# Second-stretch counting between the sort steps, warm matmuls ahead of the first bins, and all unpacking ahead of the block loop, in a graph attention kernel

## The chip, the cores and the metric

One core of a Trainium2 chip. The metric is the device time of one execution in microseconds (us), median of several runs. The span of a trace is about 1.9 us shorter than the time of the same run. The granted clock is the share of its full clock that TensorE was given; in the traces its record holds only 0.5 and 1.0, and a mean of these is given over a span.

## The reference, cut to what matters

A graph attention layer: 4096 nodes, 50000 edges, 4 heads, 64 features in and out.

```python
for h in range(n_heads):
    x_proj[h] = x @ weight[h]
    edge_scores[h] = (x_proj[h, src] * att_src[h]).sum(-1) + (x_proj[h, dst] * att_dst[h]).sum(-1)
edge_scores = np.where(edge_scores > 0, edge_scores, 0.2 * edge_scores)
# per head and destination: sum of exp(score) * x_proj[src], over the sum of exp(score) (+ 1e-8)
```

The kernel sorts the edges by source and then by destination, so that 125 destinations (one block, 33 of them) lie in a known stretch of each of 8 sorted runs. It fetches a window of each stretch, unpacks the keys into source and destination numbers (`tb`), spreads these over all partitions (`bc`), compares them to one-hot matrices (`oh`), gathers with matmuls on them (`ex`, `xs`), and sums with matmuls (`val`, `acc`).

## The kernel before

`V`, `S`, `G`, `T` are VectorE, ScalarE, GpSimd, TensorE. The part that the change touches is the hand-over from the second sort to the loop over blocks (tiny helpers cut, `...` marks cuts, the comments are added here):

```python
def unpack(self, i, *engs):                      # one window of 8 blocks: keys -> bins
    V.tensor_scalar(out=t[:, 1, :], in0=self.win[:, i, :], ...)      # source
    V.tensor_scalar(out=t[:, 0, :], in0=self.win[:, i, :], ...)      # destination
    (S.copy if i == 0 else V.tensor_copy)(out=tb[:, 1, :], in_=t[:, 1, :])
    V.tensor_scalar(out=tb[:, 0, :], in0=t[:, 0, :], scalar1=boff[:, i:i + 1], ...)
    ...                                          # stores of tb to memory, for the bc loads
...
group(so2, Lent(), ws1[:], spy)                  # second sort; then bounds(): counts -> ws2, we2
win = Windows(cst, ws2[:])                       # five indirect fetches on GpSimd
whole(so2, we2, (1 << FINE) - 1, 1)
for c in range(len(CH)):
    blocks.onehot(0, *CH[c])
    blocks.gather(0, c)
win.unpack(0, nc.sync, nc.sync)
for b in range(2, 5):
    blocks.load(b)                               # bc(2)..bc(4): loads of the stored bins
blocks.weights(0)
blocks.values(0)                                 # val: one product of 128 x 4096
for c in range(len(CH)):
    blocks.spread(1, c, win.tb[:, 0], lambda t: NT + t, S.copy if c < 2 else V.tensor_copy)
    if c == 1:
        blocks.onehot(1, *CH[0])
for c in (1, 2):
    blocks.onehot(1, *CH[c])
blocks.sums(0, -1); blocks.gather(1, 0); blocks.sums(0, 0); blocks.gather(1, 1); blocks.gather(1, 2)
win.unpack(1, nc.sync, nc.sync)
longest(so2, Lent(), (ws1, we1), (ws2, we2))     # longest stretch of all partitions
n1, n2 = room(0, EL), room(1, L)                 # two counts into registers of EVERY engine
blocks.sums(0, 1)
blocks.weights(1)
blocks.onehot(2)
blocks.run(1, {i - 1: lambda i=i: win.unpack(i, nc.sync, nc.sync) for i in range(2, NI)})
...
with tc.If((n1 > W1) | (n2 > W2)):               # fallback for long stretches: not taken here
    ...
```

## Time and profile before

| | before |
|---|---|
| time, median of 4 runs | 296.28 us (296.14 to 296.56) |
| span of the profiled run | 294.9 us, mean granted clock 0.859 |
| last result computed (`res`, VectorE) | 288.71 us |
| from there to the end of the span | 6.20 us |
| `oh` of block 2 starts | 130.87 us |

The last row divides the hand-over from the loop.

### The profile page before, as it was taken

The numbers are of one execution on the slowest core, as the hardware profiler recorded it, in microseconds if no ns is written. First come the engines' busy times: TensorE is split into PE (matmuls) and PEld (weight loads), VectorE is DVE, ScalarE is ACT, GpSimd is POOL, SyncE is SP. The second block draws the span as 40 slices with busy tenths as digits, with TensorE's granted clock in tenths as the row PEclk, the third lists the DMA queues.
The fourth block names the chain that finished last, engine by engine and source line by source line (L and its number), as shares of the span: only waits on it lengthen the run. The fifth ranks groups of instructions, "written<-read, shape, count | busy, mean of one in ns | idle before, by whom it ended". The sixth has DMA issues, their size and how long they took to land.

```text
span 294.9 us, 8453 instructions
## 1 busy us (share of the span) xinstructions
PE 202.5 (69%) x3541; PEld 193.8 (66%) x3541; DVE 260.6 (88%) x504; ACT 186.0 (63%) x361; POOL 27.6 (9%) x78
## 2 busy tenths in 40 slices
PE   0001899960000007669999999999999999999980
PEld 0000599960000005559899999999999999999980
DVE  5999999995599999679999999999999999999960
ACT  2960710040599935857778787878787778777850
POOL 7882000001100002400000000000000000000000
PEclk9999975555555555899999999999999999999996
DMA  3025000000100001295768756876578657864012
GB/s 109 0 53 109 0 2 0 0 1 37 36 0 0 0 0 40 66 392 185 242 258 307 254 185 234 292 273 197 217 289 285 197 206 282 293 203 183 8 37 59
DMA packets 13326, 40.75 MB, mean 138 GB/s; under 512 B 3120, under 2 KB 8912, under 8 KB 9312
## 3 DMA queue, kind: packets, MB, share of 16 engines
q1 hardware_dynamic: 10768, 37.91, 36.4%
q10 hardware_dynamic: 1808, 1.56, 2.3%
q0 software_dynamic: 704, 0.66, 1.0%
q8 instruction: 30, 0.49, 0.7%
q14 instruction: 16, 0.13, 0.1%
HBM read 35.08 MB, written 5.05 MB: 136 GB/s over the span
## 4 chain that ended last, share of the span: by engine, by line
PE 50%; DVE 40%; issue 3%; DMA 2%; ACT 2%; DVEq 0%; POOL 0%; POOLq 0%; ACTq 0%
PE acc L545 17%; DVE sA L210 13%; DVE sB L210 12%; PE ps L494 10%; PE pf L606 6%; PE ps L492 6%; PE ps L498 5%; PE acc L538 4%; DVE val L520 2%; DVE sB L239 1%; DVE oh L471 1%; DMA eS<-in_edge_index_dram 1%; ACT xs L502 1%; DMA raw<-gat_sorted,wi 1%; DVE sA L199 1%
## 5 line engine op out<-in xcount | busy, mean ns | idle before, releaser
L502 ACT CAST xs<-ps 128x1200 bf16<-128x1200 f32 (+1 forms) x99 | 104.0, 1051 | 0.0
L520 DVE TENSOR_TENSOR val<-xs,wv 128x4096 bf16<-128x4096 bf16 (+1 forms) x34 | 75.4, 2220 | 1.0 <-ACT xs L502 1.0
L545 PE MATMUL acc<-xs,val 128*128 128x125 bf16 x1024 | 61.8, 218 | 1.9 <-issue 1.5
L494 PE MATMUL ps<-adb,oh 128*128 128x136 bf16 x528 | 62.6, 225 | 0.0
L492 PE MATMUL ps<-xa,oh 128*128 128x72 bf16 x528 | 59.9, 198 | 2.6 <-DVE oh L471 2.2
L545 PEld LDWEIGHTS <-val 128*128 128x128 bf16 x1056 | 58.8, 98 | 2.4 <-issue 1.7
L494 PEld LDWEIGHTS <-oh 128*128 128x128 bf16 x528 | 49.8, 99 | 0.5 <-issue 0.4
L492 PEld LDWEIGHTS <-oh 128*128 128x128 bf16 x528 | 47.6, 99 | 2.9 <-DVE oh L471 2.9
L500 ACT ACTIVATE ex<-ps 128x96 bf16<-128x96 f32 (+1 forms) x99 | 25.0, 252 | 33.0 <-PE ps L498 32.9
L471 DVE TENSOR_SCALAR oh<-bc,pF 128x4096 bf16<-128x4096 bf16 (+2 forms) x37 | 42.4, 1146 | 0.3 <-ACT bc L458 0.3
L210 DVE TENSOR_TENSOR sA<-sB 128x256 f32<-128x256 f32 (+2 forms) x104 | 37.2, 399 | 1.7
L210 DVE TENSOR_TENSOR sB<-sA 128x256 f32<-128x256 f32 (+2 forms) x98 | 35.1, 399 | 1.6
L498 PE MATMUL ps<-xa,oh 128*128 128x72 bf16 x528 | 33.7, 199 | 0.0
L292 PE MATMUL cnt_ps<-sgn,sel 128*128 128x17 f32 (+1 forms) x6 | 1.7, 390 | 41.9 <-ACT sgn L284 41.9
L292 PEld LDWEIGHTS cnt_ps<-sgn,sel 128*128 128x128 f32 x6 | 1.4, 318 | 42.0 <-issue 42.0
L498 PEld LDWEIGHTS <-oh 128*128 128x128 bf16 x528 | 26.7, 100 | 0.1
L474 DVE TENSOR_SCALAR oh<-bc,pF 128x2048 bf16<-128x2048 bf16 (+2 forms) x37 | 25.5, 689 | 0.0
L395 PEld LDWEIGHTS at_ps<-uv,xT 64*128 64x128 f32 x130 | 24.8, 298 | 0.3 <-issue 0.3
L395 PE MATMUL at_ps<-uv,xT 64*128 64x4 f32 x130 | 24.9, 328 | 0.0
L606 PE MATMUL pf<-Wbd,aT 128*128 128x128 f32 x132 | 22.7, 294 | 2.7 <-ACT aT L602 0.8
L281 ACT ACTIVATE junk<-kr,nb 128x512 f32<-128x512 f32 x33 | 23.8, 722 | 1.1
L606 PEld LDWEIGHTS pf<-Wbd,aT 128*128 128x128 f32 x132 | 17.3, 191 | 4.5 <-issue 3.4
(139 smaller groups left out, 213.6 us busy)
## 6 DMA issues: line engine op xcount, KB each, us to landing
bc<-gat_bins SPq DMA_DIRECT2D x31, 1024.0 KB, 9.0
out_dram<-res SPq DMA_DIRECT2D x32, 125.0 KB
eS<-in_edge_index_dram SPq DMA_DIRECT2D x2, 195.0 KB
eD<-in_edge_index_dram ACTq DMA_DIRECT2D x2, 195.0 KB
gat_bins<-tb SPq DMA_DIRECT2D x10, 32.0 KB
gat_sorted<-sA SPq DMA_DIRECT2D x1, 256.0 KB
gat_sorted<-ki SPq DMA_DIRECT2D x1, 256.0 KB
win<-gat_sorted,wi POOLq DMA_INDIRECT x5, 2.6
```

The source lines that it names most:

```text
L210: V.tensor_tensor(out=av(d[:], o, [2 * h, n], [1, h]), in0=av(s[:], 0, [2 * h, n], [1, h]), in1=av(s[:], h, [2 * h, n], [1, h]), op=op)
L395: T.matmul(out=ps[:, b, :], lhsT=xT[:, b * step:b * step + P], rhs=uv[:, k, :], start=(b == 0), stop=True, skip_group_check=True)
L471: V.tensor_scalar(out=oh[:, 0:2, e], in0=bc[:, :, e], scalar1=pF[:, 0:1], scalar2=None, op0=OP.is_equal)
L474: V.tensor_scalar(out=oh[:, 2, e], in0=bc[:, 1, e], scalar1=pF[:, 1:2], scalar2=None, op0=OP.is_equal)
L492: T.matmul(out=ps[:, i, P:P + XC], lhsT=oh[:, 1, e], rhs=xa[:, 2 * t, :], start=(i % 2 == 0), stop=False, skip_group_check=True)
L494: T.matmul(out=ps[:, i, 0:S0], lhsT=oh[:, 0, e], rhs=adb[:, b, :], start=False, stop=False, skip_group_check=True)
L498: T.matmul(out=ps[:, i, P:P + XC], lhsT=oh[:, 2, t * W2:(t + 1) * W2], rhs=xa[:, 2 * t + 1, :], start=False, stop=True, skip_group_check=True)
L500: S.activation(out=av(ex[:], 2 * t0, [2, n], [2 * NT, 2 * H], [1, 2]), in_=av(ps[:], P, [PW, n], [1, 2 * H], [0, 2]), func=ACTF.Exp)
L502: S.copy(out=xs[:, t0:t0 + n, 0:P + XC], in_=ps[:, 0:n, 0:P + XC])
L520: V.tensor_tensor(out=av(val[:], h * Dout, [Dout, n], [C, NT], [1, Din]), in0=av(xs[:], S0, [0, n], [XW, NT], [1, Din]), in1=av(wv[:], h * ...
L545: T.matmul(out=self.to[k], lhsT=val[:, t, k * P:(k + 1) * P], rhs=xs[:, t, 0:BD], start=apart and t == 0, stop=(t == NT - 1), skip_group_c ...
L606: T.matmul(out=self.pf[b // 2][:, b % 2, k * P:(k + 1) * P], lhsT=self.aT[b // 2][:, b % 2, k * BD:k * BD + P], rhs=Wbd[:, k, :], start=(b ...
```

## The change

Three things. The counting of the second stretches is cut into single instructions and put between the last steps of the sort, where it should cost little (in the kernel before, steps around three such instructions start 0.87 and 0.95 us apart instead of 0.795). Five matmuls of 512 columns keep TensorE busy ahead of the first spreading, so that the gathers of block 0 find the full clock (in the kernel before it was half from 41.24 to 119.74). All unpacking and the reading of the two counts are moved ahead of the loop, so that the loop's first blocks have less to do. Two smaller things ride along: a copy of the first `tb` goes from ScalarE to VectorE, and `oh` of block 2 is put ahead of `wv` of block 1. The core of the diff (comments added):

```diff
-                if m == 2 and 1 << j == W2 and spy:
-                    todo = spy(self.a[self.cur])
+                todo = list(between) if m == 2 else []      # one closure after each sort step
...
+        if between:
+            warm = pp.tile([P, L], F32, name="warm")
+            for i in range(5):
+                T.matmul(out=warm[:], lhsT=identb[:], rhs=adb[:, 0:4, 0:P], start=True, stop=True)
...
-        store(skey2, so.runs(ki, FINE, spy))
-        bounds(pool, cps, 8 * NI, L, off2, m8, 8, ws2, we2)
-        whole(pool, ws2, 0, 0)
+        store(skey2, so.runs(ki, FINE, [lambda keys: st.count(), *(between or (quiet, quiet)),
+                                        *(lambda keys, f=f: f() for f in st.steps(0))]))
...
-            (S.copy if i == 0 else V.tensor_copy)(out=tb[:, 1, :], in_=t[:, 1, :])
+            V.tensor_copy(out=tb[:, 1, :], in_=t[:, 1, :])
...
         for c in range(len(CH)):
             blocks.onehot(0, *CH[c])
             blocks.gather(0, c)
+        stretches.rest()                                  # the rest of the counting
+        longest(so2, Lent(), (ws1, we1), (ws2, we2))
+        n1, n2 = room(0, EL), room(1, L)
         win.unpack(0, nc.sync, nc.sync)
...
-        win.unpack(1, nc.sync, nc.sync)
-        longest(so2, Lent(), (ws1, we1), (ws2, we2))
-        n1, n2 = room(0, EL), room(1, L)
+        for i in range(1, NI):
+            win.unpack(i, nc.sync, nc.sync)
         blocks.sums(0, 1)
+        blocks.onehot(2)
         blocks.weights(1)
-        blocks.onehot(2)
-        blocks.run(1, {i - 1: lambda i=i: win.unpack(i, nc.sync, nc.sync) for i in range(2, NI)})
+        blocks.run(1)
```

More of the change, by code (lines that the diff above doesn't have):

```diff
@@ L239, in turn, with runs @@
             V.transpose(out=d[:], in_=s[:])
-        def runs(self, to=None, fine=0, spy=None):
+        def runs(self, to=None, fine=0, between=()):
             s, d = self.step()
@@ L261, in runs @@
                 last = fine if m == 2 else 0
-                todo = []
+                todo = list(between) if m == 2 else []
                 for j in range(8, last - 1, -1):
@@ L265, in runs @@
                     if todo:
-                        todo.pop(0)()
-                    if m == 2 and 1 << j == W2 and spy:
-                        todo = spy(self.a[self.cur])
+                        todo.pop(0)(self.a[self.cur])
                 assert not todo
@@ L308, in bounds, with __init__, count, steps @@
                                 in1=av(off[:], i, [0, ni]), op=OP.add)
-    def whole(pool, t, up, what):
-        i = pool.tile([P, NI], I32, name=f"whole{what}")
-        V.tensor_scalar(out=i[:], in0=t[:], scalar1=float(up), scalar2=None, op0=OP.add)
-        V.tensor_scalar(out=i[:], in0=i[:], scalar1=FINE, scalar2=FINE, op0=OP.logical_shift_right,
-                        op1=OP.logical_shift_left)
-        V.tensor_copy(out=t[:], in_=i[:])
+    class Stretches:
+        def __init__(self, pool, ps):
+            self.ps = ps
+            self.cnt = pool.tile([P, 8 * NI + 1], F32, name="cnt")
+            self.pick = [pool.tile([P, NI, 8], F32, name=f"pick{o}") for o in range(2)]
+            self.sum = [pool.tile([P, NI], F32, name=f"sum{o}") for o in range(2)]
+            self.at = [pool.tile([P, NI], I32, name=f"at{o}") for o in range(2)]
+            self.to = [pool.tile([P, NI], I32, name=f"to{o}") for o in range(2)]
+        def count(self):
+            V.tensor_scalar(out=self.cnt[:], in0=self.ps[:], scalar1=-0.5, scalar2=RUN * L / 2, op0=OP.mult,
+                            op1=OP.add)
+        def steps(self, o):
+            up = o * ((1 << FINE) - 1)
+            return (lambda: V.tensor_tensor(out=self.pick[o][:], in0=av(self.cnt[:], o, [8, NI], [1, 8]),
+                                            in1=av(m8[:], 0, [0, NI], [1, 8]), op=OP.mult),
+                    lambda: V.tensor_reduce(out=self.sum[o][:], in_=self.pick[o][:], axis=AX, op=OP.add),
+                    lambda: V.tensor_scalar(out=self.at[o][:], in0=self.sum[o][:], scalar1=off2[:, 0:1],
+                                            scalar2=float(up), op0=OP.add, op1=OP.add),
+                    lambda: V.tensor_scalar(out=self.to[o][:], in0=self.at[o][:], scalar1=FINE, scalar2=FINE,
+                                            op0=OP.logical_shift_right, op1=OP.logical_shift_left))
+        def rest(self):
+            for f in self.steps(1):
+                f()
+            for t, i in ((ws2, self.to[0]), (we2, self.to[1])):
+                V.tensor_copy(out=t[:], in_=i[:])
     def longest(pool, pp, *sides):
@@ L336, in fetch @@
         w = start.shape[1]
-        wi = pool.tile([P, w], I32, name=f"wi{what}")
-        V.tensor_copy(out=wi[:], in_=start)
+        if start.dtype == I32:
+            wi = start
+        else:
+            wi = pool.tile([P, w], I32, name=f"wi{what}")[:]
+            V.tensor_copy(out=wi, in_=start)
         for i in range(w):
@@ L341, in fetch, with group @@
                                  in_offset=bass.IndirectOffsetOnAxis(ap=wi[:, i:i + 1], axis=1))
-    def group(pool, pp, start, spy=None):
+    def group(pool, pp, start, between=()):
         raw = pool.tile([P, L], F32, name="raw")
@@ L351, in group @@
         so.rows(9)
-        cps = counts(pool, pp, sgn, 8 * NI, [sel2[:]])
+        st = Stretches(pool, counts(pool, pp, sgn, 8 * NI, [sel2[:]])[0])
+        if between:
+            warm = pp.tile([P, L], F32, name="warm")
+            for i in range(5):
+                T.matmul(out=warm[:], lhsT=identb[:], rhs=adb[:, 0:4, 0:P], start=True, stop=True)
         ki = pool.tile([P, L], I32, name="ki")
-        store(skey2, so.runs(ki, FINE, spy))
-        bounds(pool, cps, 8 * NI, L, off2, m8, 8, ws2, we2)
-        whole(pool, ws2, 0, 0)
+        quiet = lambda keys: None
+        store(skey2, so.runs(ki, FINE, [lambda keys: st.count(), *(between or (quiet, quiet)),
+                                        *(lambda keys, f=f: f() for f in st.steps(0))]))
+        return st
     def tables(pr, pps, pp1):
@@ L558, in start, with run @@
             self.weights(0)
-        def run(self, first=0, also={}):
+        def run(self, first=0):
             for b in range(first, ND):
@@ L580, in run @@
                 self.sums(b, 1)
-                if b in also:
-                    also[b]()
             self.sink.project(ND - 1)
@@ L694, with relative, split @@
         tb0 = so2.tile([P, 2, W2], BF16)
-        def spy(keys):
-            def relative():
-                V.tensor_scalar(out=kb0[:], in0=keys[:, 0:W2], scalar1=goff[:, 0:1], scalar2=None, op0=OP.add)
-            def split():
-                V.tensor_scalar(out=t0[:, 0, :], in0=kb0[:], scalar1=8, scalar2=None, op0=OP.logical_shift_right)
-                V.tensor_scalar(out=t0[:, 1, :], in0=kb0[:], scalar1=SG - 1, scalar2=None, op0=OP.bitwise_and)
-                S.copy(out=tb0[:], in_=t0[:])
-                for c in range(len(CH)):
-                    blocks.spread(0, c, tb0[:], lambda t: RUN * t, S.copy)
-            relative()
-            return [split]
-        group(so2, Lent(), ws1[:], spy)
-        win = Windows(cst, ws2[:])
-        whole(so2, we2, (1 << FINE) - 1, 1)
+        def relative(keys):
+            V.tensor_scalar(out=kb0[:], in0=keys[:, 0:W2], scalar1=goff[:, 0:1], scalar2=None, op0=OP.add)
+        def split(keys):
+            V.tensor_scalar(out=t0[:, 0, :], in0=kb0[:], scalar1=8, scalar2=None, op0=OP.logical_shift_right)
+            V.tensor_scalar(out=t0[:, 1, :], in0=kb0[:], scalar1=SG - 1, scalar2=None, op0=OP.bitwise_and)
+            S.copy(out=tb0[:], in_=t0[:])
+            for c in range(len(CH)):
+                blocks.spread(0, c, tb0[:], lambda t: RUN * t, S.copy)
+        stretches = group(so2, Lent(), ws1[:], (relative, split))
+        win = Windows(cst, stretches.to[0][:])
         for c in range(len(CH)):
@@ L748 @@
                 with tc.tile_pool(name="sort3", bufs=1) as so3, tc.tile_pool(name="pp3", bufs=1, space=PSUM) as pp3:
-                    group(so3, pp3, at1[:])
-                    whole(so3, we2, (1 << FINE) - 1, 1)
+                    group(so3, pp3, at1[:]).rest()
                     longest(so3, pp3, (ws2, we2))
```

## The prediction

> **What bounds the kernel now.** I read the page first (busy rows and slices), then the chain of waits in order of time, then the timelines of VectorE, ScalarE, TensorE and SyncE between 104 and 165 us, because the diff touches nothing outside that stretch. The kernel has three parts: two sorts on VectorE (to 113 us), a hand-over in which the first blocks are prepared (113 to 132 us), and the loop over the other 32 blocks.
>
> ```profile
> PE   0001899960000007669999999999999999999980
> DVE  5999999995599999679999999999999999999960
> PEclk9999975555555555899999999999999999999996
> ```
>
> Each digit is 7.4 us. The sort leaves TensorE empty and its granted clock at half; in the slices of the hand-over (16 and 17) both engines have idle time; after that both read 9. In the loop the chain runs along TensorE only ("PE acc L545 x32" again and again, starts 155.57, 165.29, 175.01: 9.72 us for two blocks, 4.86 each). VectorE needs about 4.64 of the 4.86 (val 2.28, oh 1.2 + 0.67, wv 0.13, half of inv and res 0.36), so it has little to spare. The loop's first blocks, in the table by windows (columns: width, PE, PEld, DVE, ACT, POOL busy):
>
> ```profile
> 137.04:141.96 4.92, 4.88 (x104) 4.74 (x102) 4.92 (x10) 3.90 (x8) 0.00 (x0) 1.00 0.42 130
> 141.96:147.59 5.63, 5.21 (x109) 4.98 (x106) 5.63 (x11) 3.82 (x7) 0.00 (x0) 1.00 0.68 238
> 147.59:152.40 4.81, 4.81 (x105) 4.76 (x103) 4.81 (x10) 3.82 (x7) 0.00 (x0) 1.00 0.76 295
> ```
>
> One block takes 5.63 us instead of 4.86, VectorE full in it and TensorE short of work. That is where unpacking inside the loop shows.
>
> The hand-over, from VectorE's timeline (start, duration, line, tile):
>
> ```profile
> 113.12 0.19 DVE L301 TENSOR_SCALAR cnt<-cnt_ps 128x41 f32<-128x41 f32 x1
> ...
> 115.52 0.17 DVE L316 CAST we<-whole 128x5 f32<-128x5 int32 x1
> 115.60 0.61 DVE L471 TENSOR_SCALAR oh<-bc,pF 128x1536 bf16<-128x1536 bf16 x1
> ...
> 118.85 0.23 DVE L416 TENSOR_SCALAR t<-win 128x128 int32<-128x128 int32 x1 [0.79 <-DMA win<-gat_sorted,wi]
> ...
> 129.15 0.41 DVE L327 TENSOR_REDUCE most<-mx_ps 1x2 int32<-1x256 f32 x1 [0.36 <-PE mx_ps L326]
> 130.72 0.23 DVE L512 TENSOR_TENSOR wv<-ex 128x128 bf16<-128x128 bf16 x1 [1.16 <-ACT xs L502]
> 130.87 1.28 DVE L471 TENSOR_SCALAR oh<-bc,pF 128x4096 bf16<-128x4096 bf16 x1
> ```
>
> Fourteen tiny counting instructions hold VectorE from 113.2 to 115.7, after the last sort step; only then do the first one-hot tiles start, and TensorE's first gather at 116.28. At 129.6 to 130.7 VectorE reads two counts into registers (the gap is named ACT, but xs was done at 130.1). The second one-hot at 130.87 then lets the loop's first gather start at 132.21.
>
> [...] gathers from 116.28 on, clock 0.50 for 3.42 us, full from 119.7. [...] counting instructions that need the one before start 0.20 to 0.23 us apart, independent ones 0.08. [...] The warm tile borrows the single pf bank that holds the counts, so by the pool's bookkeeping the warm matmuls must follow the instruction that reads the counts; no trace shows this yet. [...] last bins store issued until 122.24, the load that reads it issued at 124.17, 1.93 later.
>
> **The change part by part.**
>
> (a) Counting between the sort steps. Three inserted instructions (kb and two t, 128 wide) are already there; the steps around them start 0.87 and 0.95 us apart instead of 0.795, so each costs about 0.08 because it fills the latency between dependent steps. The new ones (41 and 5 wide) are shorter: I give all five 0.05 together. After the last step only a 5-wide one remains: VectorE is ready for oh at about 113.45, not 115.6. But the tiles it compares come from ScalarE: bc copies run 112.12 to 115.82, ending at about 113.6, 114.9, 115.8. And TensorE's first gather needs the PSUM buffer that the second copy frees. So the first gather starts at about 115.0, not 116.28: **1.3 us** of the 2.1 arrive.
>
> (b) Warming. The count is read right after the first step, at about 108.4; five matmuls of 512 columns follow. Twelve of 256 took 2.72 us cold (0.227 each), so 0.45 each, 2.2 us, ending at 110.65, just when tb arrives for the spreads (110.64 before). TensorE is then busy from 108.4 to 114.6 with one gap of 0.25. [...] If so the gathers of block 0 run warm: 12 pairs at 0.09 us instead of 0.172, plus shorter third parts. ScalarE then paces (ex and xs 1.27, 1.27, 0.95): last xs at about 119.5 instead of 121.44. If it stays cold: 120.1. It does not shorten the spreads much, since ScalarE's copies pace them.
>
> (c) Window fetch. wi is ready 1.8 us earlier, but the store of ki still leaves at 113.4, its data end at 115.1, and GpSimd started 0.8 after its release with the first fetch (wi 71.5, start 72.33). So the fetch stays near 116.1 and win near 118.85: **0**.
>
> (d) Counts into registers, moved ahead of the first unpack. The rest of the counting takes 1.1 us after oh (116.56 to 117.5), the maxima 0.65 (118.15), then two transposes behind block 0's gathers, 0.55 (118.75 warm, 119.8 cold), the reduce 0.42 and two register loads 1.1 on every engine. Unpack 0 starts at 120.4 warm or 121.35 cold, against 118.85 now: a **new wait**, which partly replaces the 2.5 us that VectorE idles there now. The last bins store of block group 0 is issued until 122.25 warm (now 122.24, as it waits for ScalarE's tb) or 123.2 cold; bc(2) lands 4.7 after its load: 128.9 or 129.8.
>
> (e) From unpack 0 to oh(1). Warm: tb at 121.0 instead of 121.63, val ends 123.45, bc(1) copies 122.0 to 124.8, oh(1) ends 127.07 instead of 127.66 (0.6 gained). Cold: about 128.0 (0.35 lost).
>
> (f) From there to oh(2): now 3.2 us (one unpack 0.6, maxima and reduce 1.3 with waits, registers 1.15, wv 0.15). After: four unpacks of 0.55, 2.2 us. oh(2) starts at 129.27 warm, 130.2 cold, just behind the landing of bc(2). The loop's first gather follows 1.26 later: 130.5 or 131.45, against 132.21. **1.7 or 0.75 us** gained.
>
> (g) In the loop three unpacks of 0.52 to 0.6 go. TensorE's pace stays 4.86; only the block of 5.63 gets shorter, by **0.8 us**. The eight bins stores now stand ahead of bc(5) in SyncE's queue (8 x 0.61 = 4.9 us of issue), so bc(5) lands near 138; it is needed near 143.
>
> Sum: warm 1.7 + 0.8 = 2.5; cold 0.75 + 0.8 = 1.55; with 0.8 to 0.2 (rounded down for doubt to 0.75 to 0.25) 2.3. 296.27 - 2.3 = **294.0 us**, 0.8%.
>
> **The rivals.** First: nothing is lost on the way, and the 2.1 us of counting plus 1.15 of registers plus 0.8 of the loop all come through: 4 us, 292.2. Against it: ScalarE's copies and the landing of win are not moved. Second: the counts into registers, now ahead of the bins, delay the bc loads, and oh(2) waits for bc(2) (landing at 130.5 or later): only about 1 us, 295.3. For it: bc(2) would land within 0.4 of its use. Third: VectorE is the bound of the loop's head, so the three unpacks ahead of it cost their 1.65 there and the loop returns 0.8: this is in my sum, but if the loop returned nothing it would be 294.8. Fourth: the warm matmuls come late (or wait for the count longer) and delay the spreads: some 0.5 us back.
>
> **Range and chances.** 292.8 to 295.3: the low end is warm plus half of what the first rival adds, the high end is the second rival. Runs agree within 0.2 us. To be faster by 2% it would need 5.9 us, more than all removed parts together: 0.02. Slower by 2% has no mechanism here: 0.01. Within 2%: 0.97.
>
> **What would show each step.** (a) First gather at 115.0, first oh near 113.6 and waiting for bc copies. (b) Five 512-wide matmuls at 108.4, clock full before 115.3. (c) win fetch still near 116.1. (d) VectorE idle ahead of the first unpack, released by the registers and not by win; unpack 0 near 120.4. (f) oh(2) at 129.3, loop's first gather at 130.5, with or without a wait for bc(2). (g) No block over 4.95 us. The prediction is wrong if the win fetch moves, if oh(2) waits for bc(2) by more than 0.5 us, or if the loop's pace differs from 4.86.

The forecast: 2.5 us gained if the gathers run warm, 1.55 if cold. The chances of 0.8 and 0.2, rounded to 0.75 and 0.25, are the author's estimate; with them the sum came to 2.3 us, and the time to 294.0.

## More of the kernel before

TensorE's timeline (start, duration, line, instruction, and in brackets the idle time before it and what ended it):

```profile
119.83 0.29 PE L498 MATMUL ps<-xa,oh 128*128 128x72 bf16 x4
121.68 1.47 PE L456 MATMUL ps<-tb,identb 128*128 128x256 bf16 x12 [1.56 <-ACT tb L419]
```

Between the last gather of block 0 and the spreading of block 1's bins TensorE is idle for 1.56 us, and it then runs at full clock. And from the page, the packets that it lists under queue q14 as `instruction`:

```profile
q14 instruction: 16, 0.13, 0.1%
```

## The result, and the profile after

The changed kernel takes 297.62 us (297.56 to 297.89, 4 runs) against 296.28 before: ratio 1.0046, 95% interval 1.0028 to 1.0063. So it is within 2%, but slower, where 0.8% faster was predicted, and the time lies outside the predicted range. (Every ratio in this document is the mean time of one kernel's fast runs over that of the other's in the same rounds, so not quite the ratio of the medians.)

| | before | after | e13, see below |
|---|---|---|---|
| span of the profiled run | 294.9 | 295.7 | 292.7 |
| first gather of block 0 | 116.28 | 114.85 | 114.83 |
| spreading of block 1 starts | 121.68 | 122.04 | 120.88 |
| `oh` of block 2 starts | 130.87 | 130.67 | 129.25 |
| first sums of block 4 | 148.69 | 147.97 | 146.54 |
| last `res` ends | 288.71 | 287.97 | 286.53 |
| from there to the end | 6.20 | 7.75 | 6.20 |

The two traces differ in two places. The work ends 0.74 us **earlier** instead of the expected 2.3; and the end of the program, in which nothing is computed, takes 1.55 us **longer**. -0.74 + 1.55 is the 0.8 between the spans. (The medians differ by 1.3 us, as the profiled run of before took 296.82 us, 0.5 more than its median; what that 0.5 was is open, as no quicker run of it was profiled.)

The page after:

```profile
PE   0001899960000047499999999999999999999970
PEclk9999975555555558779999999999999999999996
...
q14 instruction: 17, 0.14, 0.1%
```

In the 16th slice TensorE's clock is now up (8 where it was 5), but the two slices behind it show 7 and 7 where they showed 8 and 9: the clock was gained and lost again. And there is one instruction packet more (q14).

TensorE's timeline after, at four places:

```profile
108.28 2.29 PE L379 MATMUL warm<-adb,identb 128*128 128x512 bf16 x5 [1.98 <-DVE cnt L319]
...
114.85 0.19 PE L520 MATMUL ps<-xa,oh 128*128 128x72 bf16 x1 [0.74 <-ACT bc L486]
...
117.87 0.53 PE L346 MATMUL mx_ps<-ident,mxr 128*1 128x128 f32 x2
...
122.04 2.17 PE L484 MATMUL ps<-tb,identb 128*128 128x256 bf16 x12 [3.64 <-issue]
```

The first three lines are as predicted: the warm matmuls are on time, released by the instruction that reads the counts (`cnt`), and the first gather is short (0.19 against 0.24 to 0.31 before), as the clock is full from 112.41. The last line is not. TensorE is idle for 3.64 us; the view names no engine for it ("issue"), and the twelve matmuls take 2.17 us instead of 1.47: behind this stretch the clock is half, from 122.65 to 129.48.

VectorE's timeline after:

```profile
118.44 0.41 DVE L347 TENSOR_REDUCE most<-mx_ps 1x2 int32<-1x256 f32 x1 [0.36 <-PE mx_ps L346]
119.92 0.23 DVE L444 TENSOR_SCALAR t<-win 128x128 int32<-128x128 int32 x1 [1.08 <-issue]
...
120.34 0.51 DVE L448 TENSOR_SCALAR tb<-t,boff 128x128 bf16<-128x128 int32 x1
...
120.97 2.29 DVE L548 TENSOR_TENSOR val<-xs,wv 128x4096 bf16<-128x4096 bf16 x1
124.48 0.62 DVE L499 TENSOR_SCALAR oh<-bc,pF 128x1536 bf16<-128x1536 bf16 x1 [1.22 <-ACT bc L486]
...
127.94 0.34 DVE L502 TENSOR_SCALAR oh<-bc,pF 128x512 bf16<-128x512 bf16 x1
...
130.67 1.29 DVE L499 TENSOR_SCALAR oh<-bc,pF 128x4096 bf16<-128x4096 bf16 x1
```

The first unpack waits 1.08 us for the register reads, as predicted. `tb` is ready at 120.84. But the one-hot of block 1 waits 1.22 us for ScalarE's `bc`, and ends at 128.28, later than before (127.66). The four unpacks then fill 128.20 to 130.67.

What TensorE did in its 3.64 us is in the trace's list of single instructions (not a view of the profile, as register loads and semaphore instructions count as no work). In each engine, the reading of the two counts is two TENSOR_LOAD instructions:

```
             SyncE    ScalarE  GpSimd   VectorE  TensorE
first load   118.88   118.88   118.88   118.89   121.01
TensorE in order: 120.88 event for the spreading (L484), waits for VectorE's tb; 120.96 weight load of identb (L484);
                  121.01 TENSOR_LOAD; 121.70 TENSOR_LOAD; 122.04 first matmul of the spreading
```

The first weight load of the spreading, with the event that belongs to it, stands **ahead** of TensorE's register reads, although in the source the reads come first. The built program of TensorE has them in this order (event, weight load, two reads, first matmul), so TensorE took nothing out of turn. The event waits for `tb`, which is ready at 120.84, and the two reads (0.49 and 0.31 us, 1.03 from the first one's start to the matmul) start only behind it, at 121.01. What four engines did beside VectorE's wait, TensorE did after it.

The loop's first blocks after, in the table by windows (as in the prediction):

```profile
133.41:138.25 4.84, 4.84 (x104) 4.75 (x102) 4.84 (x5) 3.82 (x8) 0.00 (x0) 1.00 0.36 101
138.25:143.25 5.00, 4.87 (x103) 4.76 (x101) 4.52 (x7) 4.10 (x8) 0.00 (x0) 1.00 0.92 344
143.25:147.97 4.72, 4.72 (x104) 4.71 (x102) 4.60 (x5) 3.53 (x8) 0.00 (x0) 1.00 1.02 375
```

The block of 5.63 is gone. From there on both kernels have the same periods, 4.71 and 5.01 in turn.

The end of the program, in the waits of SyncE's queue (line, what was waited for, us in total, times, longest), before:

```profile
SPq L799 <- PEq L799: 0.7, 2, 0.5
```

and after:

```profile
SPq L821 <- ACTq L765: 1.5, 1, 1.5
SPq L821 <- PEq L821: 0.7, 2, 0.5
```

The upper line is new. After the branch over the fallback, ScalarE's first two closing semaphore instructions stood at 292.54 and 292.63 before, and at 291.72 and 294.50 after: between two instructions that follow each other, 2.78 us. The added q14 packet starts at 295.17, behind this gap; three others start in it, at 292.32 to 292.71. What ScalarE waited for the trace does not show.

### The profile page after: what moved, and what is told of

The parts are those of the page before. It is cut to its first block, busy times and chain, and to the rows that moved or that the text cites. A ratio compares the mean times of both kernels' runs of the same rounds, so it can differ in the third digit from the quotient of the medians.

```text
span 295.7 us, 8464 instructions
## 1 busy us (share of the span) xinstructions
PE 204.9 (69%) x3546; PEld 195.1 (66%) x3546; DVE 260.2 (88%) x502; ACT 185.7 (63%) x360; POOL 29.3 (10%) x78
## 4 chain that ended last, share of the span: by engine, by line
PE 54%; DVE 36%; issue 3%; DMA 2%; ACT 2%; DVEq 0%; POOL 0%; POOLq 0%; ACTq 0%
PE acc L573 18%; DVE sA L210 12%; DVE sB L210 11%; PE ps L522 10%; PE pf L632 7%; PE ps L520 6%; PE ps L526 5%; PE acc L566 5%; DVE sB L239 1%; ACT bc L486 1%; DMA eS<-in_edge_index_dram 1%; PE ps L484 1%; DVE oh L499 1%; DMA raw<-gat_sorted,wi 1%; DVE sA L199 1%
## 5 line engine op out<-in xcount | busy, mean ns | idle before, releaser
L573 PE MATMUL acc<-xs,val 128*128 128x125 bf16 x1024 | 62.6, 220 | 0.0
L573 PEld LDWEIGHTS <-val 128*128 128x128 bf16 x1056 | 59.6, 99 | 0.1
```

The source lines that it names most:

```text
L573: T.matmul(out=self.to[k], lhsT=val[:, t, k * P:(k + 1) * P], rhs=xs[:, t, 0:BD], start=apart and t == 0, stop=(t == NT - 1), skip_group_c ...
```

## The experiments

Theories at the start: **(A)** the reads of the counts on TensorE stand behind a waiting weight load and delay the spreading; **(B)** the lost clock is what matters; **(C)** the end is longer because of the number of compiled instructions in ScalarE's program (852 instead of 855); how that would come about is not shown. Rivals are named in each expectation. A warning on times: on the chips of the later runs the kernel before itself took 295.9 to 300.6 us, its slower runs with a mean granted clock of 0.84 instead of 0.86, so single times tell little. All ratios below are against the kernel before, whose rounds hold such slower runs and so flatter a variant a little (by the medians e13 is 0.5% and not 0.7% faster, e11 1.3% and not 1.4%); the changed kernel itself was not run again beside its variants. All runs were correct.

**e1.** One idle ScalarE copy more in the changed kernel (852 to 853 instructions).

```diff
+    spare = cst.tile([P, 1], F32)
 ...
         S.copy(out=identb[:], in_=ident[:])
+        S.copy(out=spare[:], in_=ident[:, 0:1])
```

> The changed kernel plus one ScalarE instruction of one column, 60 us before anything that waits for it; no other edit. [...] ScalarE's closing instructions then lie under 0.2 us apart, the time from the last res to the end of the span falls from 7.75 to about 6.2 us, and the time from 297.6 to 296.1. The hand-over and the loop stay (first gather of the loop at 132.0). Rival: the longer end comes from the DMA or from another engine, or is the way a program ends with fewer instructions before the branch; then one column more on ScalarE changes nothing and it stays at 297.6.

Measured: 297.08 us (before 297.48 in the same rounds, ratio 0.9968, 0.989 to 1.0046). From the last `res` to the end 6.36 us, the gap at ScalarE's end gone (292.57, 292.66). In this run TensorE's clock was half from 121.10 to 131.34, 10.24 us instead of 6.83, so the work ended later (288.69), which hides the gain in the time. (C) holds for this case: one instruction that does nothing, at 19.24 us, 276 us before the end, took 1.4 us off the end.

**e2.** The kernel before with all of `tb` on VectorE, meant to give it 852 instructions.

```diff
-            (S.copy if i == 0 else V.tensor_copy)(out=tb[:, 1, :], in_=t[:, 1, :])
+            V.tensor_copy(out=tb[:, 1, :], in_=t[:, 1, :])
```

> The kernel before with one line of the change alone: the copy of tb for the first group of blocks goes from ScalarE to VectorE, so ScalarE's program is two instructions shorter, as in the changed kernel. Theory: the 2.8 us wait of ScalarE's closing instructions shows up here too, the end gets 1.5 us longer, and the time is 297.3 to 297.8 against 296.3 although tb is ready about 1.9 us sooner (what that brings the loop is at most 0.5). Rival (the end does not hang on the length of ScalarE's program): the same or 0.3 us faster than before, 296.0 to 296.3.

Measured: 297.76 us, ratio 0.9998 (0.992 to 1.0076), 6.04 us at the end. The expectation was missed through my own counting: I had counted rows of a listing; the compiled program has 853 instructions, not 852. So it says nothing against (C), and e5 repeats it properly. That the time lies in the expected 297.3 to 297.8 is luck: the end is short, but the last `res` ended at 289.84, 1.1 us later than before, in a trace whose clock was half from 132.16 to 135.57.

**e3.** Eight matmuls that wait for nothing, directly ahead of the reading of the counts in the changed kernel, to hold the clock.

```diff
+        keep = Lent().tile([P, L], F32, name="keep")
+        for i in range(8):
+            T.matmul(out=keep[:], lhsT=identb[:], rhs=adb[:, 0:4, 0:P], start=True, stop=True)
         n1, n2 = room(0, EL), room(1, L)
```

> The changed kernel with eight more matmuls of 512 columns on TensorE between the two transposes and the reading of the counts, 8 x 0.22 = 1.8 us, in the 2.5 us in which it idles there (118.4 to 120.9). Theory: the idle stretch of 3.64 us [...] costs 6.8 us at half clock (122.6 to 129.4); filled, the clock stays full. The late reading of the counts stays (spreads still start at 122.0). Then c2's copy and the second one-hot come about 0.6 to 1.0 us sooner, oh(2) starts at 129.7 to 130.1 instead of 130.67, and the time is 296.7 to 297.1 with the long end unchanged. Rival: ScalarE's copies pace this stretch whatever the clock; then oh(2) stays within 0.2 us of 130.67 and the time at 297.6.

Measured: 298.40 us, ratio 1.0021 (0.9945 to 1.0098); the clock stayed full from 113.94 to the end. Still:

```profile
122.03 1.14 PE L484 MATMUL ps<-tb,identb 128*128 128x256 bf16 x9 [1.04 <-DVE wv L540]
```

The spreading starts at 122.03 as in the changed kernel, `oh` of block 1 ends at 128.0 instead of 128.28, and `oh` of block 2 starts at 130.57 instead of 130.67. So (B) alone is not it: with the clock held, 0.1 us is gained, which is the rival's figure. The run does not test (A), as the eight matmuls themselves keep TensorE until 120.99. The last unpack waited a little: the fifth window had landed only at 129.58.

**e4.** The counts are read after the second spreading instead of ahead of unpack 0.

```diff
-        n1, n2 = room(0, EL), room(1, L)
         win.unpack(0, nc.sync, nc.sync)
 ...
             if c == 1:
+                n1, n2 = room(0, EL), room(1, L)
                 blocks.onehot(1, *CH[0])
```

> The changed kernel with the reading of the two counts into registers moved from ahead of the first unpack to after the second spread; the maxima and transposes stay. Theory: the reading stands on TensorE behind a weight load that waits for tb, so it begins only when tb is there (121.0) and costs 1.0 us on the path, after it had already cost VectorE 1.1 us ahead of the unpack. Moved, unpack 0 starts at 118.9 to 119.0, the spreads at 119.7 to 120.0, [...] the clock stays full; VectorE's reading lies largely in its wait for the bc copies. oh(2) starts at 128.6 to 129.2 and the loop's first gather at 130.0 to 130.5 instead of 132.0; with the long end unchanged the time is 295.6 to 296.2. Rival: bc(2)'s landing or ScalarE's copies take over and oh(2) stays after 130.0; time 297.0 or more.

Measured: 299.02 us, ratio 1.0044 (0.9963 to 1.0125). The hand-over gets faster as (A) wants: unpack 0 at 119.03, spreading at 120.00, `oh` of block 1 done at 126.0, 2.3 us earlier. Then all is given back:

```profile
128.12 0.23 DVE L444 TENSOR_SCALAR t<-win 128x128 int32<-128x128 int32 x1 [0.96 <-DMA win<-gat_sorted,to]
...
130.26 0.23 DVE L444 TENSOR_SCALAR t<-win 128x128 int32<-128x128 int32 x1 [1.44 <-DMA win<-gat_sorted,to]
130.87 1.28 DVE L499 TENSOR_SCALAR oh<-bc,pF 128x4096 bf16<-128x4096 bf16 x1
```

The last two unpacks wait for their windows. (Nor did the clock stay full as expected: TensorE idled from 127.63 to 132.21, the clock was half from 132.66 to 136.07, and the last `res` ended at 289.32, 1.35 us later than in the changed kernel. See e13.) This is a second limit that the changed kernel has too, hidden 0.3 us under the first: there the fifth window's data move at 126.3 to 129.7. The first four window fetches take GpSimd 0.94 to 1.01 us each in the changed kernel's trace and the fifth, which starts while VectorE runs `val` (120.97 to 123.26), takes 2.98; here the one beside `val` (119.98 to 122.27) takes 3.00 us (GpSimd's timeline of the changed kernel):

```profile
121.10 2.98 POOL L363 DMA_INDIRECT win<-gat_sorted,to  x1 [0.30 <-issue]
```

It ends at 124.08, 0.82 us behind `val`. So the window comes late, and its data move among the loads of `bc`.

**e5.** The kernel before with ScalarE's program brought to 852: e2, and the copy of the identity on GpSimd.

```diff
-        S.copy(out=identb[:], in_=ident[:])
+        G.tensor_copy(out=identb[:], in_=ident[:])
```

> The run that should have been the second one. The length of ScalarE's compiled program is 855 instructions before, 852 in the changed kernel and in the two variants of it with a long end (7.7 and 8.1 us from the last res), 853 in the padded one (6.4) and in the kernel before with the copy moved (6.0). So that run was a step short of testing the theory. Here one more ScalarE instruction goes (the copy of the bf16 identity is made by GpSimd): 852. Theory: the kernel before now has the long end, 7.5 to 8.1 us from the last res to the end of the span, with over 2.5 us between ScalarE's first and second closing instruction. Rival: the long end belongs to something else in the changed kernel; then it stays at 6.0 to 6.4.

Measured: 299.35 us (before 297.14 in the same rounds, ratio 1.0055, 0.999 to 1.0121). From the last `res` to the end 7.96 us; ScalarE's closing instructions at 292.99 and 296.02; and the new wait is there in a kernel that has only one line of the change:

```profile
SPq L799 <- ACTq L742: 1.9, 1, 1.9
```

(C) is settled as far as it can be from here: over the fifteen kernels, the five with 852 instructions end 7.66 to 8.10 us after the last `res`, the ten with 853 to 855 end 6.04 to 6.36 after it. The pages agree: the five have 17 packets in q14, the ten have 16. Why the end is longer with 852, and what ScalarE waits for behind the branch, is not shown.

**e6.** `val` of block 0 in two halves in the changed kernel, so that a window fetch beside it (2.98 us in the changed kernel) is held for less long.

```diff
-        blocks.values(0)
+        blocks.values(0, 2)
```

> The changed kernel with block 0's val written in two VectorE instructions of half the size (and so 853 ScalarE instructions: end about 6.3 us). Theory of the fifth window fetch: GpSimd's fifth fetch takes 2.98 us instead of 0.94 because val, [...] was started 0.13 us ahead of it and holds it off until it ends; its data then move between the bc loads, 126.3 to 129.7, instead of at 123.1 to 123.8. With two halves the fetch is held only until the first half ends (about 122.2): it takes 1.9 to 2.2 us, and its data move by 125.5 in large part. The loop's start should stay within 0.3 us of 132.0, as the fetch was 0.3 us from being waited for. Rival: the fetch is slow for a reason of its own queue; then it takes 2.98 again.

Measured: 296.94 us, ratio 0.9987 (0.9921 to 1.0054). The fifth fetch takes 1.76 instead of 2.98 us, and its data move at 123.6 to 124.3, ahead of the `bc` loads. `oh` of block 2 starts at 130.60: nothing gained, as the late spreading (121.70) still holds it. (853 instructions: 6.19 us at the end.)

**e7.** The last two unpacks stay in the loop, where the kernel before had them.

```diff
 ...
-        for i in range(1, NI):
+        for i in range(1, 3):
             win.unpack(i, nc.sync, nc.sync)
 ...
-        blocks.run(1)
+        blocks.run(1, {i - 1: lambda i=i: win.unpack(i, nc.sync, nc.sync) for i in range(3, NI)})
```

> The changed kernel with unpacks 3 and 4 back in the loop (853 ScalarE instructions, so the short end). The two unpacks are 1.15 us of VectorE ahead of oh(2), and the last of them was in the two runs with a quicker hand-over held by the fifth window fetch until 129.9 to 130.3. Theory: oh(2) starts 1.0 to 1.2 us sooner, at 129.5 to 129.8 (if the clock does as in the changed kernel), the loop's first gather at 130.8 to 131.0, and the loop gives back 0.3 us or less; last res about 0.8 us sooner than in the changed kernel (287.97), and with the short end the time is 1.9 to 2.3 us under the changed kernel's. Rival: bc(2)'s landing holds oh(2) at 130 or later.

Measured: 297.29 us, ratio 0.9985 (0.9921 to 1.005). `oh` of block 2:

```profile
130.70 1.29 DVE L499 TENSOR_SCALAR oh<-bc,pF 128x4096 bf16<-128x4096 bf16 x1 [0.56 <-DMA bc<-gat_bins]
```

Without the two unpacks it waits for `bc` of block 2 instead. The rival was right: three things end close together (in the changed kernel the unpacks at 130.7, with the fifth window 0.3 us ahead of its use, and `bc(2)`, by this run, also at 130.7), so that taking away any one shows nothing. (In this run the clock was half until 131.10, as in e1, and `oh` of block 1 ended at 128.94, 0.65 later than in the changed kernel; the wait for `bc(2)` stands behind that.)

**e8.** e4, e7 and e1's copy together (854 instructions); the diffs are as above.

> All that the runs point to: counts into registers after the second spread, unpacks 3 and 4 in the loop, one ScalarE instruction of padding (854). Expected: unpack 0 at 119.0, spreads at 120.0, oh(1) done at 125.9, two unpacks to 127.1, then oh(2) waits a little for bc(2) (loads issued at 122.65, landing 4.7 to 5.2 later, at 127.4 to 127.9): 127.5 to 128.0. Loop's first gather 128.8 to 129.3, 2.7 to 3.2 us sooner than in the changed kernel; clock full; the loop gives back 0.3 to 0.6. Short end. Time 1.2 to 1.5% under the changed kernel and 0.8 to 1.1% under the kernel before of the same rounds. Rival: bc(2) lands after 129.5 (held up by the window fetches that now move beside it); then only 0.5%.

Measured: 294.82 us (293.92 to 295.64), before 297.14, ratio 0.9896 (0.9844 to 0.9948). `oh` of block 2 starts at 128.37, after a wait longer than expected:

```profile
128.37 1.29 DVE L501 TENSOR_SCALAR oh<-bc,pF 128x4096 bf16<-128x4096 bf16 x1 [1.19 <-DMA bc<-gat_bins]
```

**e9.** As e3, but the eight matmuls stand *behind* the reading of the counts. A direct test of (A): the weight load that is taken ahead of the reads is then one that waits for nothing.

```diff
         n1, n2 = room(0, EL), room(1, L)
+        keep = Lent().tile([P, L], F32, name="keep")
+        for i in range(8):
+            T.matmul(out=keep[:], lhsT=identb[:], rhs=adb[:, 0:4, 0:P], start=True, stop=True)
         win.unpack(0, nc.sync, nc.sync)
```

> The changed kernel, with eight 512-wide matmuls that wait for nothing (identity as weights, the table as the moving side, nobody reads the result) put directly BEHIND the reading of the counts into registers; in e3 the same eight stood directly ahead of it. Theory (TensorE's reading of the counts stands behind a weight load of spread(1) that waits for VectorE's tb): now the weight load that comes ahead of the reading is one that waits for nothing, so TensorE reads the counts near 118.9 like the other engines (e3: 121.0 to 121.7), runs the eight, and spread(1) starts 0.1 to 0.3 us behind tb: 121.0 to 121.2, against 122.03 in e3 and 122.04 in the changed kernel. oh(1) ends near 127.0. The clock stays full as in e3. Rival (TensorE reads late because its own queue is still full of gathers, or spread(1) waits for something else than the reading): spread(1) stays at 122.0. oh(2) starts at 130.2 to 130.6 in both, as the fifth window still lands about 129.6 and unpack 4 waits for it. ScalarE's program has 852 instructions, so the stretch from the last res to the end is 7.5 to 8.1 us, and the time is 297.0 to 298.0 on a quiet chip.

Measured: 299.12 us, ratio 1.0069 (1.0011 to 1.0127; 852 instructions, 7.85 us at the end). TensorE's two register loads start at 119.06 and 119.66, with the other engines, against 121.01 and 121.70 in the changed kernel, where TensorE had stood idle from 118.40: work that comes *behind* the reads in the source has moved them 1.95 us ahead. That is (A), shown. (e3 is not the kernel to compare with, as its eight matmuls fill TensorE until 120.99.) TensorE's timeline:

```profile
120.00 1.89 PE L742 MATMUL keep<-adb,identb 128*128 128x512 bf16 x8 [1.43 <-DVE most L347]
121.72 1.47 PE L484 MATMUL ps<-tb,identb 128*128 128x256 bf16 x12
```

The spreading starts at 121.72, not at the expected 121.0 to 121.2, because I put in too many: the eight last until then. `oh` of block 2 starts at 130.81, as the fifth window still comes late (the last unpack waits 0.64 us for it). In this run the clock fell at 132.43, which it did not in e3, and the last `res` ended at 289.26.

**e10.** e1 without the five warm matmuls.

```diff
-        if between:
-            warm = pp.tile([P, L], F32, name="warm")
-            for i in range(5):
-                T.matmul(out=warm[:], lhsT=identb[:], rhs=adb[:, 0:4, 0:P], start=True, stop=True)
```

> The changed kernel without the five warm matmuls, with the one spare ScalarE copy of e1 so that its program has 853 instructions (e1 is the kernel to compare it with). If warming brings what the prediction said, the gathers of block 0 run cold, and the last xs of block 0 comes 0.6 us later than in e1, the two transposes of the maxima about 1 us later, unpack 0 near 121.0 instead of 119.9, spread(1) near 123, and oh(2) later by 0.3 to 1.0 than in e1 [...]. Rival: ScalarE paces block 0 and the waits behind it hide the warm clock, then unpack 0 and spread(1) move by less than 0.3 us and warming brought nothing. End of the program: 6.0 to 6.4 us after the last res in both cases (853 instructions).

Measured: 296.65 us (296.58 to 297.06), ratio 0.998 (0.9925 to 1.0035). Unpack 0 at 120.04, e1 120.08. This does not tell what warming brings: in this run, with the spreads alone (busy from 110.66), the clock rose at 113.46, ahead of the first gather. In the kernel before, with the same spreads, it rose only at 119.74. It does show that the warm matmuls are not always needed; inconclusive on their worth.

**e11.** e8 with `val` in halves as in e6 (855 instructions).

> e8 with val of block 0 in two halves as in e6. Theory: the fifth window fetch is described in about 1.8 us instead of 3.0, its data moves before the bc loads instead of between them, so bc(2) lands earlier; oh(2) starts at 127.2 to 128.0 with at most 0.5 us of wait, against 128.37 with 1.19 us of wait in e8; last res about 0.5 earlier than in e8's trace (287.32), that is 286.5 to 287.1; from there 6.0 to 6.4 us to the end (855 instructions), span 292.6 to 293.4. Time against the kernel before: ratio 0.985 to 0.990. Rival: oh(2) is held by the bc loads themselves and not by the windows among them, then oh(2) stays at 128.2 to 128.5 and nothing comes of it.

(That a fetch "is described" in some time, here and in e12, means how long GpSimd's instruction for it took: 2.98 us in the changed kernel, 1.76 in e6.)

Measured: 293.08 us (292.95 to 293.18, 6 runs), before 296.82, ratio 0.9856 (0.9815 to 0.9897): the fastest kernel here, 1.4% faster than before.

```profile
127.22 1.29 DVE L501 TENSOR_SCALAR oh<-bc,pF 128x4096 bf16<-128x4096 bf16 x1
```

No wait at all is left ahead of `oh` of block 2, 3.65 us earlier than in the kernel before. The last `res` ends at 285.05, better than expected, because the clock stayed full (in e8's trace it was half from 129.62 to 133.04).

**e12.** The changed kernel in its own order, with only the two faults mended: e9 with four matmuls instead of eight, and e6.

> The changed kernel with its order kept, and only the two faults that the other runs named taken away: four 512-wide matmuls that wait for nothing behind the reading of the counts (e9, with four instead of eight, so that they end near 120.9 and not after tb), and val of block 0 in two halves so that the fifth window fetch is described in 1.8 us (e6). 853 instructions on ScalarE. If the late reading on TensorE and the late fifth window were all that kept the prediction's steps (e) and (f) from coming true, then spread(1) starts at 121.0 to 121.3, oh(1) ends at 127.0 to 127.4 (predicted 127.07), the four unpacks follow without a wait for a window, oh(2) starts at 129.3 to 129.9 (predicted 129.27), the first gather of the loop 1.34 behind it, last res 286.6 to 287.4, 6.0 to 6.4 from there to the end, and the time is 293.5 to 295.0 on a quiet chip, 0.988 to 0.993 of the kernel before. Rival: something else holds oh(2) near 130.5 (the landing of bc(2), as in e7), then the time is about that of e6, 0.997.

Measured: 296.43 us (295.86 to 297.69), ratio 0.998 (0.9935 to 1.0026). The hand-over came out as in the prediction: spreading at 120.88, `oh` of block 1 done at 126.9 (predicted 127.07), `oh` of block 2 at 129.24 (predicted 129.27), first gather of the loop at 130.57 (predicted 130.5). It took both mends: `oh` of block 2 starts at 130.67 in the changed kernel, at 130.81 with the first mend alone (e9) and at 130.60 with the second alone (e6). Yet the first sums of block 4 came at 147.78, hardly ahead of the changed kernel. TensorE's timeline and the table by windows (the column before the last two is the clock):

```profile
130.57 0.21 PE L520 MATMUL ps<-xa,oh 128*128 128x72 bf16 x1 [2.05 <-DVE oh L499]
```

```profile
128.00:130.40 2.40, 0.52 (x10) 0.35 (x7) 2.40 (x10) 1.60 (x4) 0.00 (x0) 1.00 1.03 423
130.40:132.58 2.18, 2.01 (x23) 1.86 (x24) 2.08 (x4) 0.77 (x2) 0.00 (x0) 0.69 1.01 334
132.58:138.06 5.48, 5.48 (x102) 5.47 (x101) 4.24 (x5) 3.38 (x8) 0.00 (x0) 0.81 0.64 193
```

While VectorE unpacks four windows TensorE has nothing to do for 2.05 us, and the clock is half from 131.23 to 134.64, in the loop's first blocks, where TensorE is the limit. Block 1 takes 5.48 instead of 4.84. From 130.67 to 129.24 the hand-over gained 1.43 us; 147.97 to 147.78 is 0.19; so 1.24 were lost in between.

**e13.** e12 with that idle stretch filled, to see whether the clock took it (the prediction was wrong, and this was still open).

```diff
         blocks.gather(1, 2)
+        fill = Lent().tile([P, L], F32, name="fill")
+        for i in range(8):
+            T.matmul(out=fill[:], lhsT=identb[:], rhs=adb[:, 0:4, 0:P], start=True, stop=True)
         for i in range(1, NI):
```

> e12 with eight more 512-wide matmuls that wait for nothing, behind the last gather of block 1 and ahead of the second half of the sums of block 0, so that TensorE has work from 128.5 to about 130.2 while VectorE unpacks. Theory (the gain of e12 was lost to the clock): the clock stays full through the loop's head; oh(2) at 129.2 to 129.4 and first gather at 130.5 to 130.7 as in e12; the first sums of block 1 about 0.6 earlier than in e12 (131.9 to 132.1), those of block 4 1.0 to 1.3 earlier (146.5 to 146.8), last res 286.7 to 287.0, 6.0 to 6.4 from there to the end (853 instructions), span 292.8 to 293.3, and a time of 0.990 to 0.995 of the kernel before. Rival (something else in the loop's head, the stores of the bins or the late bc loads, takes it): block 4 stays at 147.6 to 147.9 with the clock full, and the time at that of e12 (0.998).

Measured: 295.66 us (294.51 to 296.09), before 297.06, ratio 0.9926 (0.9874 to 0.9978). TensorE's timeline:

```profile
127.48 1.89 PE L761 MATMUL fill<-adb,identb 128*128 128x512 bf16 x8
129.21 1.04 PE L573 MATMUL acc<-xs,val 128*128 128x125 bf16 x16
130.59 0.21 PE L520 MATMUL ps<-xa,oh 128*128 128x72 bf16 x1 [0.33 <-DVE oh L499]
```

The clock stays full; `oh` of block 2 is where it was in e12 (129.25); the sums of block 4 come at 146.54, 1.24 us earlier than in e12, and the last `res` ends at 286.53, 2.18 us earlier than in the kernel before. With the three mends (ready matmuls behind the reads, `val` in halves, the idle stretch filled) and 853 instructions the change brings what was predicted, trace against trace: 2.18 against 2.3, and in neither trace did the clock fall in the loop's head. By the medians it is 1.4 us.

One trace each would not settle the clock's part, for the length of an idle stretch alone does not tell whether the clock falls (2.05 us in e12, where it fell): in e3 TensorE idled at the same place for 2.25 us (129.66 to 131.92) and the clock stayed full. But the other traces agree. Where all unpacks stand ahead of the loop, the last `res` ends 157.28 to 157.37 us after `oh` of block 2 starts if the clock does not fall behind it (after, e1, e3, e6, e10, e13), and 158.45 to 158.75 us if it does (e4, e9, e12).

## Why the prediction was wrong, point by point

- **(a) right.** The counting between the steps costs next to nothing (steps with one such instruction between them start 0.78 to 0.81 us apart, without one 0.795); first gather at 114.85 for 115.0.
- **(b) half right.** Matmuls at 108.28, clock full at 112.41, as predicted; that warming earns anything was not shown (e10). The working used a warm clock for block 0 and never asked whether it lasts: TensorE then idles for 3.64 us and the clock falls. Held by itself it was worth 0.1 us (e3), as the late reads and the fifth window held the rest.
- **(c) right for the first fetch,** at 116.04, before 116.12; the fifth is the matter of (f).
- **(d) right as a wait, 0.5 us too long.** Unpack 0 at 119.92 for 120.4, held by the registers and not by the window.
- **(e) failed.** The step said: registers read on every engine while VectorE waits, then `tb` at 121.0, copies from 122.0, `oh` of block 1 done at 127.07. `tb` came at 120.84, but copies began at 123.01 and `oh` was done at 128.28. TensorE's reads stood behind the weight load of the spreading, which is held until `tb` is there, and so came after it in series (121.01 for 118.9; shown by e9 against the changed kernel). In the kernel before, the same kind of weight load stood ahead of the reads too, but it was one of `val`, which was ready.
- **(f) failed, in part through (e).** Predicted 129.27, measured 130.67. The 2.2 us for four unpacks came out at 2.47. Even with (e) mended, the fifth window would have held it at 130.8 (e9): the prediction knew of the fetches only the first. Its blocking by `val` was not foreseen. In the kernel before it had been issued at 121.45, just ahead of `val` at 121.47, and took 0.94 us; in the changed kernel `val` comes 0.5 us earlier and so ahead of it. With both mended the step comes out at 129.24 (e12).
- **(g) right in kind, too large.** From `oh` of block 2 to the sums of block 4: 17.82 us before, 17.30 after, 0.5 gained for 0.8 predicted. In e12, where the hand-over is as fast as predicted, the idle stretch of 2.05 us put the half clock into this part and took 1.24 us; this was nowhere in the working. Its sign "no block over 4.95 us" was set wrongly: the undisturbed loop runs 4.71 and 5.01 in turn. The eight stores of bins took 8.8 us on SyncE and not 4.9 (128.91 to 137.67), but nothing waited for the load behind them.
- **Not in the working at all: the end of the program**, +1.55 us. The change takes three instructions from ScalarE (855 to 852), and every kernel here with 852 has the long end, whatever else it holds (e5); why is not shown. Without this the changed kernel would have been 0.2 (by the medians) to 0.7 us (by the traces) faster than before, still outside the range.

Of the rivals, none was the one. The second (a transfer delays `oh` of block 2) came nearest: the changed kernel shows no such wait, but the window and `bc(2)` stood just behind the unpacks and were the next limit in e4, e7 and e8. None of the three signs that the prediction named for being wrong came true (the first fetch, a wait for `bc(2)`, the pace). The low end of its range does not follow from its own rule, which gives 293.0; that changes nothing. Left open: what warming ahead of block 0 is worth, and why the end is longer with 852 ScalarE instructions.

## What to carry to other kernels

When a step that every engine has to make (reading a count into registers) is moved, look for what stands in each queue around it: in the built program of the changed kernel a weight load of the next matmul stood ahead of it, and TensorE made the step after the wait (121.01) instead of beside it (118.9 on the other engines); ready matmuls behind the reads mended it (119.06 in e9). In a hand-over several chains can end close together (here the unpacks and `bc(2)` at 130.7, and the fifth window 0.3 us ahead of its use, e7), so mend all that the trace shows just below the limit before judging any one, and then check the clock again: in e12 the shortened chain left TensorE idle for 2.05 us, and 1.24 of the 1.43 us won were lost. Compare the stretch from the last useful instruction to the end of the span too: here it grew by 1.55 us, where the work had gained 0.74.
